# Hybrid conformer and gated-recurrence layer: the MLP's first product with tokens stationary, its results turned by VectorE and through memory

## The chip, the core and the metric

The kernel runs on one core of one Trainium2 chip. The metric is device microseconds of one execution. The engines are called here as the profile calls them: PE is TensorE's matmuls, PEld its weight loads, DVE is VectorE, ACT is ScalarE, POOL is GpSimd, SP is SyncE, which here only issues transfers.

## The reference

One layer over 256 latent tokens of width 2048, with 256 context tokens ahead of them: a modulation from the conditioning vector, a convolution branch and a gated recurrence branch that are merged and projected, and then an MLP. The change touches the MLP alone:

```python
D_MODEL = 2048
SEQ = 256
D_FF = 4 * D_MODEL

def sq_relu_mlp(h, w1, w2):
    return jnp.square(jax.nn.relu(h @ w1)) @ w2

h2 = modulate(rms_norm(x, norm_pre_mlp[l]), sh_f, sc_f)
x = x + ga_f * rms_norm(sq_relu_mlp(h2, mlp_w1[l], mlp_w2[l]), norm_post_mlp[l])
```

h is 256 x 2048, w1 is 2048 x 8192, w2 is 8192 x 2048, all float32.

## The kernel before

**Products.** Every product is made of three, to keep float32's precision: an operand is split into a high part and the rest (hi and lo), and hi*hi, hi*lo and lo*hi are summed in PSUM. Activations are split once (`split`, L237); weights arrive as pages of 128 x 1024 (512 KB) through SP's queue (`fetch`, L85) into 5 raw buffers, ACT makes whi (L123) and DVE makes wlo (L126), each in 4 buffers. `Stream.next` keeps up to 4 pages ready ahead of PE. A raw buffer, a whi or a wlo is written again only when its reader is done.

**Two forms of a product.** In `blocks` (with `mm2`, L252 and L254) a 128 x 128 piece of the weights is stationary and the tokens move: a page is eight matmuls of 512 columns (whi against hi and lo of the 256 tokens side by side) and eight of 256 columns (wlo against hi). The result has features on the partitions, as the next product needs it for its stationary operand; its two halves of 256 columns still have to be added (`totals`: an ACT copy at L228, a DVE add at L229, for each 128 features). In `tokens` (with `mm3r`, through L185) 128 x 128 pieces of the activations are stationary and the weights move: a page is twelve matmuls of 512 columns (3 terms, 2 blocks of 128 tokens called tb, 2 halves of the page called j). The result has tokens on the partitions. Four banks fill at once; of the last three pages (LAST) each bank is finished in turn, so that the banks end one after another.

**The MLP's order.** The 8192 hidden features are four quarters q of 2048. `up(q)` makes a quarter's hidden values and `down(q)` multiplies them by their rows of w2; each takes 32 pages. `up` is of the `blocks` form, `down` of the `tokens` form. The evacuation of `up` (`ev`) takes 256 features at a time: `totals`, relu on ACT (L988), square on ACT (L990), `split` into pages hidh and hidl. The first 1024 features of `up(0)` are an exception: `first_up` makes them in the `tokens` form, page by page behind the projection that delivers its input. Their values stand with tokens on the partitions in two pages called hidden (L1202), and the generator `turn_hidden` turns them with 16 PE transposes (L1215) and splits them, while the rest of `up(0)` runs.

**Background work.** Generators are pushed on a list, and `pump` runs a step of up to three of them after each page; `finish` runs one to its end. In the MLP a generator of another kind, `gain_row`, makes rows of gains; its two transfers (L1276, L1277) are issued from POOL. The products for it (`gemv`, L1236 on DVE) come as extra raw pages, one after every sixth page of w1 and w2, up to 32.

**Buffers and order.** Pages of 128 x 1024 float32 come from one pool of 30 (`page`). Each engine, and each queue of transfers, works its own list of instructions in order; a planner makes that list when the kernel is built, from the order of the code and from what it takes to be ready, and inserts all waits. `issue_after` only orders instructions on one engine.

Of the kernel before, what the change touches and what calls it, by code (L numbers as in the profile page):

```python
# [8 lines left out]
F32 = mybir.dt.float32  # L9
F32R = mybir.dt.float32r  # L10
I32 = mybir.dt.int32
U8 = mybir.dt.uint8
AF = mybir.ActivationFunctionType
ALU = mybir.AluOpType

P = 128
T = 256
D = 2048
KT = D // P
# [7 lines left out]
TW = 1024  # L27
# [7 lines left out]
PB = 4  # L35
# [16 lines left out]
class Stream:  # L52


    def __init__(self, kn):
        self.kn = kn
        self.items = []
        self.done = 0
        self.behind = []
        self.ready = collections.deque()  # L60
        self.raws = collections.deque()
        self.dma = None
# [74 lines left out]
class Kernel:  # L137
    def __init__(self, ctx, tc, a, out):
        self.tc = tc
        self.nc = tc.nc  # L140
        self.a = a
        self.out = out
        self.wp = ctx.enter_context(tc.tile_pool(name="wp", bufs=1))
        self.pg = ctx.enter_context(tc.tile_pool(name="pg", bufs=1))
        self.sp = ctx.enter_context(tc.tile_pool(name="sp", bufs=1))
        self.cp = ctx.enter_context(tc.tile_pool(name="cp", bufs=1))
        self.ps = ctx.enter_context(tc.tile_pool(name="ps", bufs=1, space=bass.MemoryType.PSUM))
        self.bg = collections.deque()
        self.his, self.los = [], []
        self.credit = 0.0  # L150
        self.queued = None
# [213 lines left out]
    def run(self):  # L365
        nc, a = self.nc, self.a
# [125 lines left out]
        first = self.cp.tile([P, 1], F32, name="first")  # L492
# [9 lines left out]
        for i in range(2):  # L502
            ps = self.bank()
# [160 lines left out]
        for c in range(8):  # L664
            part = sums(c, self.last3)
            ps = self.bank()
            for t in range(KP // 2):
                st.fetch_to(FETCH)
                w = st.whole()
                for k2 in range(2):  # L670
                    k = 2 * t + k2
                    g = 32 * (k % 4)
# [69 lines left out]
        for h in range(NH):  # L742
            accs = []
            for d in range(2 * (h > 0)):
                accs.append(self.bank())
                for hf in range(2):
                    hi, lo = st.next()
                    for k8 in range(8):
                        k = 8 * hf + k8
# [18 lines left out]
        uh = self.pages(2, F32, "uh")  # L768
# [201 lines left out]
        h2x = self.operand(h2)  # L970
        y2 = self.pages(4, F32, "y2")
        hid = {}
        begun = self.first_up(yp, xr, A2, mv[:, 0], h2)
        self.tokens(zx, ev_wo, 1.4, end=True, pre=pre_wo, begin=begun)


        def up(q):
            uh_, ul_ = [], []
            hid[q] = (uh_, ul_)

            def ev(b, acc):
                if b % PB == 0:
                    uh_.append(self.page(F32R, "hidh"))
                    ul_.append(self.page(F32R, "hidl"))
                if isinstance(acc, list):
                    acc = self.totals(acc, self.small(512, "sum"))
                r = self.small(512, "relu")
                nc.scalar.activation(out=r, in_=acc, func=AF.Relu)  # L988
                sq = self.small(512, "rsq")
                nc.scalar.activation(out=sq, in_=r, func=AF.Square)  # L990
                self.split(sq, self.at(uh_, b, 2), self.at(ul_, b, 2))
            if q == 0:
                for n in range(2):
                    uh_.append(self.page(F32R, "hidh"))
                    ul_.append(self.page(F32R, "hidl"))
                turned = self.push(self.turn_hidden(uh_, ul_))
            self.blocks(16 if q else 8, h2x, KT, ev, 1.4, first=0 if q else 8)
            if q == 0:
                self.finish(turned)

        def gained2(yp, tb, c, s=slice(0, 512)):
            nc.vector.tensor_tensor(self.cut(yp, tb, c)[:, s], self.cut(y2, tb, c)[:, s], gain_row(1, c)[:, s], op=ALU.mult)

        def down(q):
            uh_, ul_ = hid[q]

            def ev(tb, c, acc):
                y = self.cut(y2, tb, c)
                if q == 0:
                    nc.scalar.copy(out=y, in_=acc)  # L1010
                    return
                end = (tb, c) == (1, 3) and q == 3
                nc.vector.tensor_tensor(y, acc[0] if end else acc, y, op=ALU.add)
                if q < 3:
                    return
                if not end:
                    self.squares(ssq[:, 4 * tb + c:4 * tb + c + 1], y)
                    gained2(yp, tb, c)
                else:

                    for h in range(2):
                        s, o = slice(h * T, (h + 1) * T), ssq[:, 7 + h:8 + h]
                        nc.vector.tensor_tensor(y[:, s], acc[1 + h], y[:, s], op=ALU.add)
                        if h == 0:
                            self.squares(o, y[:, s])
                            gained2(yp, tb, c, s)
                        else:
                            nc.vector.scalar_tensor_tensor(self.small(T, "junk"), y[:, s], 1.0, y[:, s], op0=ALU.mult, op1=ALU.mult, accum_out=o)
                if c < 3:
                    return  # L1030
                r = self.rstd_tok(ssq[:, 4 * tb:4 + 5 * tb])[0]
                if end:
                    with self.tc.issue_after(self.summed.ins):
                        gained2(yp, tb, c, s)
                for i in range(4):
                    x1, o = self.cut(xr, tb, i), self.out[tb * P:(tb + 1) * P, i * 512:(i + 1) * 512]
                    if end and i == 0:

                        halves = [(self.bank()[:, :T], slice(h * T, (h + 1) * T)) for h in range(2)]
                        for ps, s in halves:  # L1040
                            nc.tensor.matmul(ps, v["ident"], x1[:, s], start=True, stop=False)
                        self.warm(10)
                        diag = self.small(P, "diag")
                        nc.scalar.activation(out=diag, in_=v["ident"], func=AF.Copy, scale=r)
                        for ps, s in halves:
                            nc.tensor.matmul(ps, diag, self.cut(yp, tb, i)[:, s], start=False, stop=True)
                        for ps, s in halves:
                            nc.scalar.copy(out=x1[:, s], in_=ps)
                            nc.scalar.dma_start(o[:, s], x1[:, s])
                        continue  # L1050
                    for s in (slice(0, T), slice(T, 512)) if end and i in (1, 3) else (slice(0, 512),):
                        nc.vector.scalar_tensor_tensor(x1[:, s], self.cut(yp, tb, i)[:, s], r, x1[:, s], op0=ALU.mult, op1=ALU.add)
                        nc.sync.dma_start(o[:, s], x1[:, s])
            yp = self.pages(4, F32, "gained") if q == 3 else None
            self.tokens(lambda k: (self.at(uh_, k), self.at(ul_, k)), ev, 1.4, end=q == 3, halves=q == 3)

        for q in range(4):
            up(q)
            down(q)

    def first_up(self, y, x, A, B, h2):
# [4 lines left out]
        nc, st = self.nc, self.stream  # L1066
        ident = self.v["ident"]
# [50 lines left out]
        t = {}  # L1118
# [32 lines left out]
        for k in range(2):  # L1151
            a, b = cols(k)
# [18 lines left out]
        for k in range(FIRST, KT):  # L1171
            pair = 4 if k == FIRST else k + 2 if k % 2 == 0 else KT
            if pair < KT:
                ps = self.bank()
# [19 lines left out]
                        self.add(0, slice(0, T), False)  # L1194
            self.pump(1.4)

        self.hidden = [self.page(F32, "hidden") for tb in range(2)]
        for tb in range(2):
            for j in range(2):
                r = self.small(512, "relu")  # L1200
                nc.scalar.activation(out=r, in_=accs[tb][j], func=AF.Relu)
                nc.scalar.activation(out=self.hidden[tb][:, j * 512:(j + 1) * 512], in_=r, func=AF.Square)  # L1202

    def split_at(self, src, parts, t):
        return self.split(src, parts[:, t], parts[:, T:][:, t])

    def turn_hidden(self, uh, ul):

        for _ in range(3):
            yield None  # L1210
        for b in range(0, 8, 2):
            ps = self.bank()
            for j in range(2):
                for tb in range(2):
                    self.nc.tensor.transpose(out=ps[:, j * T + tb * P:j * T + (tb + 1) * P], in_=self.hidden[tb][:, (b + j) * P:(b + j + 1) * P], identity=self.v["ident"])  # L1215
            self.split(ps, self.at(uh, b, 2), self.at(ul, b, 2))
            yield 0.7
            yield None

    def warm(self, n=WARM):  # L1220

        ps = self.bank()
        for _ in range(n):
            self.pe(self.nc.tensor.matmul, ps[:, :P], self.ones_r, self.ones_r, start=True, stop=True)

    def gemv(self, raw, i, k, h):

# [396 lines left out]
```

## Time and profile before

| | |
|---|---|
| median of 3 runs | 1643.5 us (1642.47 to 1644.42) |
| the profiled execution | 1644.45 us |
| its span in the profile | 1642.7 us, so 1.75 us lie around it |
| granted clock of TensorE | full in all slices |
| PE / DVE / ACT busy | 99% / 71% / 49% of the span |

A page of the profile gives busy times of the engines, the chain of work that ended last, and groups of instructions by source line with a mean duration and what ended the idle time before them. Matmuls are pipelined, so a matmul's own duration is longer than its share of PE's time; what one costs is read from the distance between starts, or from a stretch divided by its count.

### The profile page before, as it was taken

Reading aid. Unit: us, or ns where it says so; the run is one execution under the profiler, and the core shown is the slowest. Engines: PE = TensorE matmul, PEld = TensorE weight load, DVE = VectorE, ACT = ScalarE, POOL = GpSimd, SP = SyncE. Lnnn points to the kernel's source line nnn. Section 1 sums busy time; section 2 is a strip of 40 time slices with the busy share of each in tenths; the row PEclk is TensorE's granted clock in tenths of the full one; section 3 lists DMA queues with packets and bytes.
Section 4 is the critical chain, followed back from the end, with each engine's and each line's share of the span. In section 5 each row is a group of like instructions: output and inputs, shape, how many; then the busy total and the mean of one; then the engine's idle time right before and its main releaser. Section 6 shows DMA issues by size and latency. Waiting matters only on the chain.

```text
span 1642.7 us, 22019 instructions
## 1 busy us (share of the span) xinstructions
PE 1627.8 (99%) x8211; PEld 1359.2 (83%) x8211; DVE 1163.1 (71%) x1703; ACT 799.9 (49%) x1142; POOL 8.1 (0%) x18
## 2 busy tenths in 40 slices
PE   8999999999999999999999999999999999999998
PEld 6668888888988888888888888888888888888887
DVE  7777777778868889967887766456655665566555
ACT  6553444443554444653446665445544554346543
POOL 0000000000000000000000000000000000000000
PEclk9999999999999999999999999999999999999999
DMA  9998954444656556688887376677667667666553
GB/s 375 389 395 292 318 163 149 154 142 141 204 185 227 189 187 210 228 277 294 317 291 269 136 233 204 212 237 240 219 205 232 233 214 215 232 219 195 190 192 116
DMA packets 103771, 374.47 MB, mean 228 GB/s; under 512 B 11632, under 2 KB 12400, under 8 KB 103664
## 3 DMA queue, kind: packets, MB, share of 16 engines
q1 hardware_dynamic: 102096, 368.60, 66.4%
q0 software_dynamic: 1280, 4.21, 0.9%
q8 instruction: 64, 1.05, 0.3%
q14 instruction: 43, 0.35, 0.1%
q10 hardware_dynamic: 288, 0.26, 0.0%
HBM read 370.93 MB, written 2.10 MB: 227 GB/s over the span
## 4 chain that ended last, share of the span: by engine, by line
PE 93%; DVE 2%; DMA 2%; ACT 1%; issue 1%; SPq 0%; ACTq 0%; DVEq 0%
PE bank L185 62%; PE bank L252 18%; PE bank L254 9%; PE bank L1396 2%; DMA raw<-wpw 1%; DVE wlo L126 1%; DMA x<-ctx 1%; DMA rawpage<-wm 1%; ACT whi L123 0%; PE bank L1427 0%; PE bank L1438 0%; PE bank L1436 0%; DVE gacc L1236 0%; SPq L498 0%; PE bank L1419 0%
## 5 line engine op out<-in xcount | busy, mean ns | idle before, releaser
L126 DVE TENSOR_TENSOR wlo<-raw,whi 128x1024 fp32r<-128x1024 f32 x488 | 594.7, 1224 | 356.2 <-ACT whi L123 348.4
L123 ACT ACTIVATE whi<-raw 128x1024 fp32r<-128x1024 f32 x488 | 513.4, 1059 | 577.7 <-PE bank L185 322.9
L185 PE MATMUL bank<-whi,h 128*128 128x512 f32 x1264 | 396.6, 392 | 0.8 <-ACT h L629 0.5
L252 PE MATMUL bank<-h,whi 128*128 128x512 f32 x1280 | 322.4, 394 | 0.0
L185 PEld LDWEIGHTS bank<-whi,h 128*128 128x128 f32 x1264 | 237.3, 188 | 50.9 <-DVE h L1085 0.7
L252 PEld LDWEIGHTS bank<-h,whi 128*128 128x128 f32 x1280 | 230.7, 189 | 41.3
L185 PE MATMUL bank<-wlo,h 128*128 128x512 f32 x632 | 246.9, 391 | 0.7 <-DVE wlo L126 0.5
L185 PE MATMUL bank<-whi,hidh 128*128 128x512 f32 x503 | 195.3, 388 | 0.0
L185 PE MATMUL bank<-wlo,hidh 128*128 128x512 f32 x503 | 195.3, 388 | 0.0
L185 PE MATMUL bank<-whi,hidl 128*128 128x512 f32 x503 | 195.3, 388 | 0.0
L254 PEld LDWEIGHTS bank<-h,wlo 128*128 128x128 f32 x1280 | 174.6, 190 | 12.6
L254 PE MATMUL bank<-h,wlo 128*128 128x256 f32 x1280 | 178.5, 283 | 0.0
L185 PE MATMUL bank<-h,whi 128*128 128x512 f32 x512 | 164.7, 403 | 0.0
L185 PEld LDWEIGHTS bank<-wlo,h 128*128 128x128 f32 x632 | 118.8, 188 | 26.5 <-DVE wlo L126 2.4
L185 PEld LDWEIGHTS bank<-whi,hidh 128*128 128x128 f32 x503 | 94.5, 188 | 19.3
L185 PEld LDWEIGHTS bank<-whi,hidl 128*128 128x128 f32 x503 | 94.5, 188 | 19.2
L185 PEld LDWEIGHTS bank<-wlo,hidh 128*128 128x128 f32 x503 | 94.5, 188 | 19.2
L185 PEld LDWEIGHTS bank<-h,whi 128*128 128x128 f32 x512 | 92.1, 189 | 21.4 <-issue 5.9
L185 PE MATMUL bank<-h,wlo 128*128 128x512 f32 x256 | 100.2, 391 | 0.0
L1236 DVE SCALAR_TENSOR_TENSOR gacc<-raw,silu_c,gacc 128x1024 f32<-128x1024 f32 x60 | 76.8, 1279 | 0.0
L1249 DVE SCALAR_TENSOR_TENSOR raw<-raw,silu_row 128x1024 f32<-128x1024 f32 x64 | 76.5, 1220 | 0.0
L185 PEld LDWEIGHTS bank<-h,wlo 128*128 128x128 f32 x256 | 48.1, 188 | 10.5 <-DVE wlo L126 0.3
(246 smaller groups left out, 1363.0 us busy)
## 6 DMA issues: line engine op xcount, KB each, us to landing
raw<-w SPq DMA_DIRECT2D x256, 512.0 KB, 4.3
raw<-wi SPq DMA_DIRECT2D x172, 512.0 KB, 4.4
raw<-wmt SPq DMA_DIRECT2D x64, 512.0 KB, 4.3
raw<-wm SPq DMA_DIRECT2D x64, 512.0 KB, 4.5
rawpage<-wm SPq DMA_DIRECT2D x48, 512.0 KB, 8.8
raw<-wo SPq DMA_DIRECT2D x32, 512.0 KB, 4.7
raw<-wmd SPq DMA_DIRECT2D x16, 512.0 KB, 8.6
raw<-who SPq DMA_DIRECT2D x16, 512.0 KB, 5.1
```

What stands on the lines that cost most here:

```text
L123: kn.his.append(nc.scalar.activation(out=hi, in_=raw, func=AF.Copy))
L126: kn.los.append(nc.vector.tensor_tensor(lo, raw, hi.bitcast(F32), op=ALU.subtract))
L185: ins = fn(*args, **kw)
L252: nc.tensor.matmul(bank, w[0][:, cut(i)], x(k)[2], start=(k == 0), stop=False)
L254: nc.tensor.matmul(bank[:, T:], w[1][:, cut(i)], x(k)[0], start=False, stop=(k == nk - 1))
L1236: nc.vector.scalar_tensor_tensor(acc, raw, s, acc, op0=ALU.mult, op1=ALU.add)
L1249: nc.vector.scalar_tensor_tensor(raw, raw, 1.0, self.srow, op0=ALU.mult, op1=ALU.mult, accum_out=self.dot[:, 32 * j + b:32 * j + b + 1])
L1396: nc.tensor.matmul(ps[:, b * P:(b + 1) * P], w, r, start=True, stop=True)
```

## The change

`up(q)` is written in the `tokens` form throughout: the pieces of h2 are stationary and w1's pages move, laid out as w2's are. Its four evacuations for each 1024 features do relu and square on ACT, as before, and then `turn_blocks`: a DVE transpose of a 128 x 512 piece in blocks of 32 x 32, written into a page called turned. When both pages (one for each tb) of 1024 features are there, `turn_hidden` is pushed. Its first step, `swapped`, sends each page to a buffer in DRAM (one transfer of 512 KB) and fetches it back in four transfers of 128 KB, each to 32 partitions in runs of 1 KB, which puts the 32 x 32 blocks in their places; all ten are issued from POOL. After five empty steps it splits the fetched pages into hi and lo, in a step for each tb (two ACT and two DVE instructions of 128 x 512). For the first 1024 features of a quarter this runs during the second half of `up(q)`, and `up` finishes it at its end. For the second 1024 it runs beside the first pages of `down(q)`, which finishes it ahead of its page 7; the features are needed from page 8 on. `first_up` uses the same way, and the PE transposes are gone.

```diff
+        turns = {0: [self.push(self.turn_hidden(hid, 0, self.hidden))]}
+
         def up(q):
-            uh_, ul_ = [], []
-            hid[q] = (uh_, ul_)
-
-            def ev(b, acc):
-                if b % PB == 0:
-                    uh_.append(self.page(F32R, "hidh"))
-                    ul_.append(self.page(F32R, "hidl"))
-                if isinstance(acc, list):
-                    acc = self.totals(acc, self.small(512, "sum"))
+            def ev(tb, c, acc):
+                if c % 2 == 0:
+                    self.hidden[tb] = self.page(F32, "turned")
                 r = self.small(512, "relu")
                 nc.scalar.activation(out=r, in_=acc, func=AF.Relu)
                 sq = self.small(512, "rsq")
                 nc.scalar.activation(out=sq, in_=r, func=AF.Square)
-                self.split(sq, self.at(uh_, b, 2), self.at(ul_, b, 2))
-            if q == 0:
...
-            self.blocks(16 if q else 8, h2x, KT, ev, 1.4, first=0 if q else 8)
-            if q == 0:
-                self.finish(turned)
+                self.turn_blocks(self.hidden[tb], c % 2, sq)
+                if (tb, c % 2) == (1, 1):
+                    turns.setdefault(q, []).append(self.push(self.turn_hidden(hid, q, list(self.hidden))))
+            self.hidden = [None, None]
+            self.tokens(h2x, ev, 1.4, groups=2 if q else 1)
+            self.finish(turns[q][0])
...
+            def pre(g, k):
+
+                if (g, k) == (0, 7):
+                    self.finish(turns[q][1])
...
+    def turn_blocks(self, page, j, src):
+        out = page[:, :TW].rearrange("p (j b r) -> p b j r", j=4, b=8)[:, 4 * j:4 * j + 4]
+        self.nc.vector.transpose(out=out, in_=src.rearrange("p (b j r) -> p b j r", b=4, j=4))
...
+    def turn_hidden(self, hid, q, pages):
...
+        for tb in range(2):
+            back.append(self.swapped(pages[tb]))
+        for _ in range(5):
             yield None
-        for b in range(0, 8, 2):
-            ps = self.bank()
-            for j in range(2):
-                for tb in range(2):
-                    self.nc.tensor.transpose(...)
-            self.split(ps, self.at(uh, b, 2), self.at(ul, b, 2))
-            yield 0.7
-            yield None
+        new = [[self.page(F32R, f"hid{n}") for i in range(2)] for n in "hl"]
+        for p, pages in zip(parts, new):
+            p.extend(pages)
+        for tb in range(2):
+            for n in range(2):
...
+                with self.tc.issue_after(self.his[-1].ins):
+                    self.split(src, hi, lo)
+            yield 1.4
...
+    def swapped(self, page):
+        there = self.dr.tile([P, TW], F32, name="there", tag="there", bufs=4)
+        nc.gpsimd.dma_start(there, page[:, :TW])
+        back = self.page(F32, "back")[:, :TW]
+        for j in range(4):
+            nc.gpsimd.dma_start(back[32 * j:32 * j + 32].rearrange("c (i f) -> c i f", i=4),
+                                there[:, j * T:(j + 1) * T].rearrange("(i c) f -> c i f", i=4))
+        return back
```

## Rows read from the trace of the kernel before

**Rows 1.** The page: busy us (share of the span) and instructions of each engine.
```profile
PE 1627.8 (99%) x8211; PEld 1359.2 (83%) x8211; DVE 1163.1 (71%) x1703; ACT 799.9 (49%) x1142; POOL 8.1 (0%) x18
```
**Rows 2.** Who PE waited for, longest first: us in total, times, longest.
```profile
PE bank L185 <- DVE silu_c L391: 4.5, 1, 4.5
PE bank L185 <- DMA x<-x: 2.3, 1, 2.3
```
**Rows 3.** Stages: the rest of up(0), down(0), up(1), down(2), up(3).
```profile
core 0: us, PE busy (x) PEld busy (x) DVE busy (x) ACT busy (x) POOL busy (x), PEclk, DMA share, GB/s
969.18:1015.62 46.44, 46.44 (x273) 41.09 (x272) 28.60 (x32) 29.16 (x43) 0.00 (x0) 1.00 0.67 217
1015.62:1102.69 87.07, 87.07 (x386) 72.14 (x385) 43.48 (x38) 37.97 (x43) 1.05 (x2) 1.00 0.69 223
1102.69:1192.05 89.36, 89.36 (x513) 78.71 (x512) 56.99 (x61) 51.50 (x71) 0.00 (x0) 1.00 0.70 224
...
1369.41:1456.48 87.07, 87.07 (x387) 72.12 (x385) 48.05 (x45) 33.96 (x36) 0.00 (x0) 1.00 0.67 217
1456.48:1546.76 90.28, 90.28 (x517) 79.45 (x516) 57.20 (x64) 52.16 (x72) 0.00 (x0) 1.00 0.63 205
```
**Rows 4.** The tile hidden: PE transposes (ns min/median/max, first and last start).
```profile
L1215 PE MATMUL bank<-pack,hidden x16: 272/273/274, 980.3 to 990.4; 128*128 128x128 f32 x16
```
**Rows 5.** Groups by line in the whole span: busy us, mean ns, idle before.
```profile
L229 DVE TENSOR_TENSOR sum<-bank,terms 128x256 f32<-128x256 f32 x72 | 30.1, 418 | 5.3 <-ACT terms L228 5.3
...
L237 DVE TENSOR_TENSOR hidl<-rsq,hidh 128x512 fp32r<-128x512 f32 x28 | 19.3, 691 | 0.3 <-ACT hidh L237 0.3
L988 ACT ACTIVATE relu<-sum 128x512 f32<-128x512 f32 x28 | 17.7, 633 | 36.7 <-DVE sum L229 36.7
...
L990 ACT ACTIVATE rsq<-relu 128x512 f32<-128x512 f32 x28 | 17.3, 617 | 0.2
```
**Rows 6.** Timeline where down(1) ends and up(2) begins: start, duration, engine, line.
```profile
1276.17 0.69 DVE L1013 TENSOR_TENSOR y<-bank,y 128x512 f32<-128x512 f32 x1 [1.16 <-PE bank L185]
...
1278.21 0.69 DVE L1013 TENSOR_TENSOR y<-bank,y 128x512 f32<-128x512 f32 x1 [1.35 <-PE bank L185]
...
1278.89 2.96 ACT L123 ACTIVATE whi<-raw 128x1024 fp32r<-128x1024 f32 x3 [5.74 <-PE bank L185]
...
1279.98 2.36 DVE L126 TENSOR_TENSOR wlo<-raw,whi 128x1024 fp32r<-128x1024 f32 x2 [1.08 <-ACT whi L123]
1280.05 1.98 PE L252 MATMUL bank<-h,whi 128*128 128x512 f32 x8
1280.28 0.50 POOL L1276 DMA_DIRECT2D bias<-bgain  x1 [187.68 <-PE bank L185]
1280.79 0.55 POOL L1277 DMA_DIRECT2D gain<-gain  x1
...
1282.26 0.69 DVE L1013 TENSOR_TENSOR y<-bank,y 128x512 f32<-128x512 f32 x1
```
**Rows 7.** Line L1277 from 1270 to 1290 us: its one transfer, 512 KB.
```profile
DMA to landing us min/median/max: 4.9/4.9/4.9
```
**Rows 8.** Line L855, four transfers of 512 KB from POOL.
```profile
DMA to landing us min/median/max: 4.6/5.9/7.7
```
**Rows 9.** The page's list of transfers: KB each, median us from issue to landing.
```profile
gain<-gain POOLq DMA_DIRECT2D x4, 512.0 KB, 6.1
...
out<-xr SPq DMA_DIRECT2D x4, 128.0 KB, 2.4
```
**Rows 10.** Two stretches of 5 us behind the end of down(1), columns as in the stages.
```profile
1281.00:1286.00 5.00, 5.00 (x31) 4.47 (x30) 4.27 (x6) 3.05 (x4) 0.34 (x1) 1.00 0.70 240
1286.00:1291.00 5.00, 5.00 (x31) 4.38 (x30) 3.93 (x4) 1.80 (x3) 0.00 (x0) 1.00 1.02 413
```
**Rows 11.** POOL's timeline in the MLP.
```profile
1081.39 0.50 POOL L1276 DMA_DIRECT2D bias<-bgain  x1 [268.13 <-PE bank L185]
```
**Rows 12.** Line L1234, the one DVE operation of the MLP with a scalar operand.
```profile
L1234 DVE TENSOR_SCALAR gacc<-raw,silu_c x4: 747/750/757, 679.4 to 1216.8; 128x1024 f32<-128x1024 f32 x4
```

More of the change, by code (lines that the diff above doesn't have):

```diff
@@ L146, in __init__ @@
         self.cp = ctx.enter_context(tc.tile_pool(name="cp", bufs=1))
+        self.dr = ctx.enter_context(tc.tile_pool(name="dr", bufs=1, space=bass.MemoryType.DRAM))
         self.ps = ctx.enter_context(tc.tile_pool(name="ps", bufs=1, space=bass.MemoryType.PSUM))
@@ L990, in ev @@
                 nc.scalar.activation(out=sq, in_=r, func=AF.Square)
-                self.split(sq, self.at(uh_, b, 2), self.at(ul_, b, 2))
-            if q == 0:
[L993 to L996, printed above, removed]
-            self.blocks(16 if q else 8, h2x, KT, ev, 1.4, first=0 if q else 8)
-            if q == 0:
-                self.finish(turned)
+                self.turn_blocks(self.hidden[tb], c % 2, sq)
[4 more added lines that the diff above has]
+            self.finish(turns[q][0])
         def gained2(yp, tb, c, s=slice(0, 512)):
@@ L1054, in down @@
             yp = self.pages(4, F32, "gained") if q == 3 else None
-            self.tokens(lambda k: (self.at(uh_, k), self.at(ul_, k)), ev, 1.4, end=q == 3, halves=q == 3)
+            self.tokens(lambda k: (self.at(uh_, k), self.at(ul_, k)), ev, 1.4, end=q == 3, halves=q == 3, pre=pre)
         for q in range(4):
@@ L1195, in first_up @@
             self.pump(1.4)
-        self.hidden = [self.page(F32, "hidden") for tb in range(2)]
+        self.hidden = [self.page(F32, "turned") for tb in range(2)]
         for tb in range(2):
@@ L1201, in first_up @@
                 nc.scalar.activation(out=r, in_=accs[tb][j], func=AF.Relu)
-                nc.scalar.activation(out=self.hidden[tb][:, j * 512:(j + 1) * 512], in_=r, func=AF.Square)
+                sq = self.small(512, "rsq")
+                nc.scalar.activation(out=sq, in_=r, func=AF.Square)
+                self.turn_blocks(self.hidden[tb], j, sq)
     def split_at(self, src, parts, t):
         return self.split(src, parts[:, t], parts[:, T:][:, t])
-    def turn_hidden(self, uh, ul):
-        for _ in range(3):
-            yield None
-        for b in range(0, 8, 2):
-            ps = self.bank()
-            for j in range(2):
-                for tb in range(2):
-                    self.nc.tensor.transpose(out=ps[:, j * T + tb * P:j * T + (tb + 1) * P], in_=self.hidden[tb][:, (b + j) * P:(b + j + 1) * P], identity=self.v["ident"])
-            self.split(ps, self.at(uh, b, 2), self.at(ul, b, 2))
-            yield 0.7
-            yield None
+    def turn_blocks(self, page, j, src):
+        out = page[:, :TW].rearrange("p (j b r) -> p b j r", j=4, b=8)[:, 4 * j:4 * j + 4]
+        self.nc.vector.transpose(out=out, in_=src.rearrange("p (b j r) -> p b j r", b=4, j=4))
+    def turn_hidden(self, hid, q, pages):
+        nc = self.nc
+        parts = hid.setdefault(q, ([], []))
+        back = []
+        for tb in range(2):
+            back.append(self.swapped(pages[tb]))
+        for _ in range(5):
+            yield None
+        new = [[self.page(F32R, f"hid{n}") for i in range(2)] for n in "hl"]
[3 more added lines that the diff above has]
+            for n in range(2):
+                src = back[tb].rearrange("p (i b r) -> p b i r", i=4, b=8)[:, PB * n:PB * n + PB]
+                hi, lo = (pages[n][:, :TW].rearrange("p (b t i r) -> p b t i r", b=PB, t=2, i=4)[:, :, tb] for pages in new)
+                with self.tc.issue_after(self.his[-1].ins):
+                    self.split(src, hi, lo)
+            yield 1.4
     def warm(self, n=WARM):
@@ L1224, in warm @@
             self.pe(self.nc.tensor.matmul, ps[:, :P], self.ones_r, self.ones_r, start=True, stop=True)
+    def swapped(self, page):
+        nc = self.nc
+        there = self.dr.tile([P, TW], F32, name="there", tag="there", bufs=4)
[5 more added lines that the diff above has]
+        return back
     def gemv(self, raw, i, k, h):
@@ L1575, in rows @@
         return w.reshape(n, P, 2, TW).transpose(2, 0, 1, 3).reshape(-1, P, TW)
-    def both(w):
-        n = w.shape[0] // P
-        return np.concatenate([w[:, :TW].reshape(n, P, TW), cb(w[:, TW:])], axis=0)
     def row(w):
@@ L1611 @@
         "wo": rows(f(w_out)[0]),
-        "w1": np.concatenate([both(w1[:, :D]), cb(w1[:, D:])], axis=0),
+        "w1": np.concatenate([rows(w1[:, i * D:(i + 1) * D]) for i in range(4)], axis=0),
         "w2": np.concatenate([rows(w2[i * D:(i + 1) * D]) for i in range(4)], axis=0),
```

## Prediction

> **What bounds the kernel now.** I read the page first: PE is busy for 1627.8 us, 99% of the span, DVE 71%, ACT 49% [rows 1]. Then PE's waits: the two longest, 4.5 and 2.3 us, lie at the very start of the kernel, and every later one is 0.5 us or less [rows 2]. Then the stages of the MLP one by one: in each of them PE is busy for the whole stretch, at the full clock, with DVE at 50 to 64% of it, ACT at 39 to 63% and the transfers at 63 to 70% of theirs [rows 3]. So in the MLP the time is PE's, and only two things change it: what PE's own instructions take, and whether anything makes PE wait where it never waits now.
>
> **What PE saves.** A quarter of `up` and a quarter of `down` are both 32 pages with the same products, in the two forms. down(0) and down(2) take 87.07 us each, 2.721 us for a page of twelve matmuls, 226.7 ns for one. up(1) takes 89.36 us, 2.793 us for a page [rows 3]. The columns that move are the same (8 x 512 + 8 x 256 against 12 x 512); the difference is sixteen instructions against twelve. So up(1), up(2) and up(3) lose 2.29 us each, 6.87 us together (up(3)'s 90.28 holds a product for a gain row, which stays). The rest of up(0) is 16 pages and the 16 PE transposes, 46.44 us [rows 3, 4]; in the new form it is 16 x 2.721 = 43.53 us, so 2.91 us less, of which half of 2.29 is the form and 1.76 the transposes. Together **9.78 us**. The price of the new form is not a guess by analogy: `down` runs it on the same chip with the same shapes. I take it whole; below it could be nothing (a rival), above it nothing speaks for more.
>
> **What the other engines get.** DVE loses 56 adds of `totals` at 418 ns (23.4 us) and ACT 56 copies; DVE gets 32 transposes of 128 x 512. The trace has none. The nearest rows of that size are 691 ns (a subtraction with two inputs [rows 5]) and, halved, the 750 ns of a scalar operation on twice the size, 375 ns [rows 12]; at the upper end I put twice the former, 1.38 us, since an output in strides may cost more. I take 0.69: 22.1 us, as much as goes away. Even at 1.38 us DVE stays under 70% in a stage of 87 us, so this is hidden by PE's work. Relu, square and the splits stay as many (relu 633 ns, square 617 [rows 5]) but for four more splits. The evacuation is no wait for PE: four banks fill while the other four are emptied, as in `down`. POOL, nearly idle (8.1 us [rows 1]), gets 80 issues of some 0.53 us. The transfers get 16 pages out and back, 16.8 MB over some 670 us, 25 GB/s on the 205 to 224 that flow there [rows 3]; the weights have five raw buffers and four pages ready in front of PE, some 10 us of cover, so a landing later by a microsecond or two costs nothing.
>
> **What is new on PE's path.** The first 1024 features of each quarter are turned while PE works 16 pages of `up`, 43.5 us; that covers any price below. The second 1024 are not: they exist when `up(q)` ends, and `down(q)` wants them at its page 8. There are four such places. Let 0 be the end of `up`. I build the time L at which the last fetched piece lands.
>
> The end of down(1) shows what an end of this form looks like [rows 6]. Banks end 2.04 us apart (1276.17 to 1278.21 were such evacuations), so tb 0's second bank ends at -4.1, and its page is turned after relu, square and transpose (1.25 + 0.69) at about -2 to -1. tb 1's last bank ends at 0. ACT has three whi queued to 1281.85, that is 1.8 after the end, and DVE two wlo to 2.3 (which is why the last y stands at 1282.26). So tb 1's page is ready between 2.2 and 3.8; I take 3.8.
>
> A POOL issue takes 0.50 to 0.55 us. The price of a transfer is best read at the very same place: the 512 KB that POOL issued at 1280.79 landed after 4.9 us [rows 6, 7]. The medians elsewhere are 6.1 [rows 9] and 5.9, the extremes of the latter group 4.6 and 7.7 [rows 8]; a 128 KB transfer of 1 KB runs took 2.4 where nothing else ran [rows 9]. Weights do run here: the transfers are busy 0.70 and then all of the time in the two stretches behind the boundary [rows 10]. I take 4.9 for each step, also for the four pieces back, which are 512 KB together; bounds 2.4 and 7.7.
>
> Two orders on POOL are possible. If the second page goes out before the first comes back: 3.8 + 4.9 = 8.7 out, the last of four pieces issued at 10.3, L = 15.2. If POOL waits for the first page's return before it issues the second: -1 + 4.9 = 3.9, four issues to 6.0, out at 10.9, last piece issued 12.5, **L = 17.4**; with 6.1 a step 21.0; with 7.7 a step 25.8; with 2.4 a step about 10. What the code's order says is the second; I take it.
>
> When is L too late? PE reaches page 8 at 8 x 2.72 = 21.8, and wants tb 1's lo at 23.6 at the earliest; it is there at L + 0.63 + 0.69, so L may be 22.2. A tighter limit is ACT's queue: the splits of tb 1 stand behind the whi of page 8 and ahead of that of page 9. While ACT waits for L, page 9 waits too: two splits (1.26), whi (1.0), wlo (1.2) make L + 3.5, and PE wants that wlo at 24.7. So **L may be 21.2**, and each microsecond beyond costs PE one, four times. The taken 17.4 leaves 3.8 us; the stall is nothing. Its cover is PE's pages 0 to 8 of `down`, and if that cover is gone the price is (L - 21.2) x 4.
>
> One rule of the Trainium skill speaks against POOL as the issuer. The row first: at 1280.28 and 1280.79, in the middle of two wlo that kept DVE busy from 1279.98 to 1282.34, POOL's issues took 0.50 and 0.55 us [rows 6], so a DVE subtraction with two inputs doesn't hold them. The Trainium skill (SBUF — State Buffer, section SBUF: two separate sides) says that a transfer issued from GpSimd has its descriptors written by GpSimd, which is locked out while VectorE runs an operation that takes both ports, and advises the other queues. Whether the transpose is such an operation it doesn't say there, and no row here can show it. By the row the sum stays; by the rule, were it so, see the third rival.
>
> **The rivals.**
>
> *1. The round trip comes late (the other side).* With each step at 7.7 us, as one row of four on POOL had it [rows 8], L = 25.8 and PE stalls 4.6 us at each of four ends: 1633.7 + 18.4 = 1652. It decides at L = 22.8 (gain within 0.2%) and at 24.5 (slower by over 0.2%): a step of 6.7 or 7.3 us in the serial order. For it: the transfers are full right behind the boundary [rows 10]. Against it: 4.9 was measured in that very stretch [rows 7]. Chances: L up to 21.2 see the forecast; 21.2 to 22.8, still faster (1634 to 1640), 0.09; 22.8 to 24.5, 0.07; above, 0.11.
>
> *2. A queue on POOL.* POOL works in order, and a transfer for a gain row once waited there 268 us until PE freed a page [rows 11]. A page on its way out that stands behind such a wait stalls PE until the page is free: behind the one that ended at 1081.39, 1081.39 - 1015.62 - 21 = some 45 us, 1679. Against it: the last such issue stood right at a boundary and held nothing [rows 6]. Chance 0.04.
>
> *3. The transposes hold POOL's issues.* Two of them, for tb 1, run when POOL issues the first page's return. At 0.69 each L is 18.8 and nothing changes; at 1.38 each with steps of 6.1, L = 23.8, a stall of 2.6 x 4 and 1644, no gain. As the third number needs both bounds at once, it has 0.03, taken as faster, since most of its cases are at 1634 to 1640. It is the rule above that gives this case.
>
> *4. The change doesn't do what it says:* the new form takes 2.79 us a page here too, and only the 1.76 us of the PE transposes is gained: 1641.7. Against it stand two stages of the same form with the same price [rows 3]. Chance 0.04.
>
> **How the numbers follow.** The profiled execution took 1644.45 us, 1.75 beyond its span; less 9.78 that is 1634.7. It lies 0.95 above the median of the runs, 1643.5, and so I predict 1643.5 - 9.78 = **1633.7 us** for the median, with 0.62 for this case and its own range of 1632.5 to 1635 (the runs spread by 1 us to each side). A measurement of this kernel tells about 0.2%, 3.3 us, from no change. Faster: 0.62 + 0.09 + 0.03 = 0.74. Same: 0.07 + 0.04 = 0.11. Slower: 0.11 + 0.04 = 0.15. The range reaches into the cases with a partly late return and takes in the fourth rival: 1632.5 to 1642, which leaves out slower and a part of the same, less than 0.2.
>
> **What would show it.** After the change each of up(1) to up(3) should take 87.1 us (up(3) 88.0) and the rest of up(0) 43.5, PE busy throughout. The transposes on DVE should read 0.4 to 1.4 us, most likely 0.7. PE's waits should stay free of any for a split of the fetched pages or for the whi and wlo of pages 8 to 10 of `down`. POOL's transfers near the four ends should land in 5 to 6 us, the last at 15 to 21 after `up`'s end. The prediction is wrong if `down` grows from 87.1 to 90 or more in all four quarters (a late return), if one quarter grows by tens of microseconds (a queue on POOL), or if `up` stays at 89.

## The result and the profile after

The changed kernel takes 1649.45 us (median of 11 runs, 1643.26 to 1653.83) against 1643.5 before: 1.0033 of the time, 95% interval 1.0021 to 1.0046. It is slower by a third of a per cent, where 1633.7 was forecast, and its runs spread by 10 us where those of before spread by 2. The profiled execution took 1651.03 us, its span is 1649.3.

The first line of the page after, beside [rows 1]:
```profile
PE 1624.1 (98%) x7747; PEld 1336.4 (81%) x7747; DVE 1162.8 (71%) x1679; ACT 780.6 (47%) x1086; POOL 52.0 (3%) x98
```
PE has less to do and is less busy: the span grew by work that is not PE's. The stages say where. The view is that of [rows 3], after the change: up(0) with its first half, down(0), up(1), down(1), down(2), up(3), and down(3) to the end.
```profile
core 0: us, PE busy (x) PEld busy (x) DVE busy (x) ACT busy (x) POOL busy (x), PEclk, DMA share, GB/s
920.75:1012.81 92.06, 91.75 (x419) 75.32 (x419) 63.55 (x92) 56.84 (x93) 6.04 (x11) 1.00 0.70 225
1012.81:1104.60 91.79, 89.24 (x385) 73.10 (x384) 47.80 (x44) 40.73 (x47) 4.91 (x9) 0.98 0.73 233
1104.60:1191.64 87.04, 87.04 (x385) 72.11 (x384) 51.52 (x48) 43.32 (x51) 6.03 (x11) 1.00 0.77 250
1191.64:1284.74 93.10, 89.88 (x389) 73.75 (x388) 55.45 (x56) 38.00 (x42) 5.99 (x11) 0.98 0.72 235
...
1371.78:1463.80 92.02, 89.11 (x385) 73.06 (x384) 52.45 (x51) 36.80 (x40) 5.99 (x11) 0.98 0.73 238
1463.80:1551.77 87.97, 87.97 (x389) 72.86 (x388) 51.98 (x51) 43.77 (x52) 6.01 (x11) 1.00 0.74 229
1551.77:1649.30 97.53, 91.07 (x421) 75.43 (x419) 58.27 (x71) 41.49 (x58) 4.92 (x9) 0.99 0.57 182
```
`up` went as forecast: 89.36 became 87.04 in up(1) (and in up(2), which repeats it), 90.28 became 87.97 in up(3), 6.95 us together. But `down`, whose products the change doesn't touch, became longer: 87.07 to 91.79 and 92.02 in down(0) and down(2), and 5.1 and 1.6 us more in down(1) and down(3), which took before:
```profile
1192.05:1280.05 88.00, 88.00 (x390) 72.89 (x389) 51.04 (x50) 35.11 (x38) 0.00 (x0) 1.00 0.66 215
...
1546.76:1642.70 95.94, 90.53 (x422) 75.58 (x420) 53.69 (x65) 38.50 (x54) 0.00 (x0) 1.00 0.48 159
```
That is 16.4 us together. The span grew by 6.6; 16.4 less 6.6 and 6.95 leaves 2.8 us that were gained ahead of down(0), close to the 2.91 of the sum for up(0) (the start of down(0) varies by 1.7 us between the runs below). So the saving is there, and well over one and a half times as much is lost at four places in `down`.

PE's waits name the places. Before, none in the MLP was over 0.5 us [rows 2]; now the longest group of the whole kernel is this:
```profile
PE bank L186 <- ACT hidh L238: 9.7, 4, 3.2
```
There are four pauses, one in each `down`, some 23 us after its start: PE waits for the split of the fetched pages, at page 8. The split waits for the last piece, as ACT's timeline in down(1) shows (starts at 1191.64):
```profile
1211.85 0.61 ACT L238 ACTIVATE hidh<-back 128x512 fp32r<-128x512 f32 x1
1217.01 0.63 ACT L238 ACTIVATE hidh<-back 128x512 fp32r<-128x512 f32 x1 [4.54 <-DMA back<-there]
```
And POOL's timeline of the trip that ends there:
```profile
1190.06 0.56 POOL L1246 DMA_DIRECT2D there<-turned  x1 [25.14 <-DVE turned L1212]
1193.51 2.19 POOL L1249 DMA_DIRECT2D back<-there  x4 [2.89 <-issue]
1196.56 0.56 POOL L1246 DMA_DIRECT2D there<-turned  x1 [0.87 <-DVE turned L1212]
1206.98 2.18 POOL L1249 DMA_DIRECT2D back<-there  x4 [9.86 <-ACT whi L123]
1209.15 0.51 POOL L1303 DMA_DIRECT2D bias<-bgain  x1
```
From issue to landing these took, in the same order, with the weights that SP issued from 1194 to 1201 us in the last line:
```profile
DMA to landing us min/median/max: 2.9/2.9/2.9
...
DMA to landing us min/median/max: 4.3/7.5/8.3
...
DMA to landing us min/median/max: 9.8/9.8/9.8
...
DMA to landing us min/median/max: 6.0/7.1/8.3
...
DMA to landing us min/median/max: 8.0/8.0/8.0
...
DMA to landing us min/median/max: 8.8/9.3/9.8
```
The first page goes out in 2.9 us, while the weights rest at the end of `up`. Then the weights start again, and most transfers take 6 to 10 us: a page out 9.8, a piece of 128 KB up to 8.3, and even a transfer of 4 KB for the gain row 8.0. It was issued behind the pieces on POOL's queue, and landed 0.2 us after the last of them. The weights themselves, which took 3.2 to 4.7 us behind the same boundary before, need 9.3. The last piece was issued at 1208.61 and took 8.30, so it lands at 1216.91, that is L = 25.3 us after the end of `up`. The stretches of 5 us in which this happens show why:
```profile
1199.00:1204.00 5.00, 5.00 (x24) 4.14 (x23) 1.79 (x2) 0.32 (x1) 0.00 (x0) 1.00 1.02 278
1204.00:1209.00 5.00, 5.00 (x24) 4.15 (x23) 3.11 (x3) 3.36 (x4) 2.02 (x4) 1.00 1.01 394
1209.00:1214.00 5.00, 5.00 (x24) 4.14 (x23) 3.02 (x3) 2.15 (x3) 1.23 (x3) 1.00 0.99 238
```
For 15 us the 16 DMA engines are busy all of the time (the column ahead of the last), where [rows 10], behind the end of a `down`, had one such stretch of 5.

What a pause costs is more than its length. The four pauses are 9.7 us and the loss is 16.4. The other 6.6 us are in PE's busy time, which in down(1) grew from 88.00 to 89.88. TensorE's granted clock (the column ahead of the DMA share) fell behind the pause that ended at 1217.69:
```profile
1216.00:1218.00 2.00, 0.31 (x1) 0.31 (x2) 0.84 (x1) 0.99 (x2) 0.00 (x0) 0.90 1.02 373
1218.00:1220.00 2.00, 2.00 (x5) 1.34 (x5) 2.00 (x4) 2.00 (x4) 0.00 (x0) 0.50 1.01 401
1220.00:1222.00 2.00, 2.00 (x8) 1.57 (x7) 2.00 (x5) 0.67 (x2) 0.00 (x0) 0.74 0.21 84
1222.00:1224.00 2.00, 2.00 (x11) 1.60 (x10) 1.80 (x3) 1.06 (x1) 0.00 (x0) 1.00 0.00 0
```
0.50 is the lower of the two levels, 1.2 GHz: from 1218 to 1220 PE starts 5 matmuls, from 1222 to 1224, at the full clock, 11. The shares 0.90, 0.50 and 0.74 leave out 0.86 x 2 = 1.7 us of the full clock.

DVE's transposes, the one operation that no trace had shown, were as taken (0.69):
```profile
L1212 DVE STREAM_TRANSPOSE turned<-rsq 128x512 f32<-128x512 f32 x32 | 22.6, 708 | 22.5 <-ACT rsq L987 22.0 <-ACT rsq L1202 0.4
```

### The profile page after: what moved, and what is told of

Same layout as the page of the kernel before. It is cut to its first block, busy times and chain, and to the rows that moved or that the text cites. A ratio compares the mean times of both kernels' runs of the same rounds, so it can differ in the third digit from the quotient of the medians.

```text
span 1649.3 us, 21098 instructions
## 1 busy us (share of the span) xinstructions
PE 1624.1 (98%) x7747; PEld 1336.4 (81%) x7747; DVE 1162.8 (71%) x1679; ACT 780.6 (47%) x1086; POOL 52.0 (3%) x98
## 4 chain that ended last, share of the span: by engine, by line
PE 85%; DMA 7%; DVE 3%; ACT 2%; issue 1%; SPq 0%; POOL 0%; ACTq 0%; DVEq 0%; POOLq 0%
PE bank L186 73%; PE bank L253 5%; PE bank L255 3%; PE bank L1423 2%; DMA back<-there 2%; DVE wlo L126 1%; DMA there<-turned 1%; DMA raw<-wpw 1%; DMA rawpage<-wm 1%; ACT whi L123 1%; DMA raw<-wf 1%; DMA x<-ctx 1%; DMA raw<-w 1%; PE bank L1454 0%; PE bank L1465 0%
## 5 line engine op out<-in xcount | busy, mean ns | idle before, releaser
L126 DVE TENSOR_TENSOR wlo<-raw,whi 128x1024 fp32r<-128x1024 f32 x488 | 592.7, 1222 | 311.9 <-ACT whi L123 305.6
L186 PE MATMUL bank<-whi,h 128*128 128x512 f32 x2160 | 673.2, 391 | 0.8 <-ACT h L630 0.5
L186 PEld LDWEIGHTS bank<-whi,h 128*128 128x128 f32 x2160 | 405.5, 188 | 86.0 <-DVE h L1084 0.7
L186 PE MATMUL bank<-wlo,h 128*128 128x512 f32 x1080 | 421.3, 390 | 0.6 <-DVE wlo L126 0.5
L186 PEld LDWEIGHTS bank<-wlo,h 128*128 128x128 f32 x1080 | 203.0, 188 | 43.7 <-DVE wlo L126 2.6
L186 PE MATMUL bank<-h,whi 128*128 128x512 f32 x512 | 164.7, 403 | 0.0
L186 PEld LDWEIGHTS bank<-h,whi 128*128 128x128 f32 x512 | 92.1, 189 | 21.4 <-issue 5.9
L253 PE MATMUL bank<-h,whi 128*128 128x512 f32 x384 | 97.8, 397 | 0.0
L253 PEld LDWEIGHTS bank<-h,whi 128*128 128x128 f32 x384 | 69.1, 189 | 12.3
L186 PEld LDWEIGHTS bank<-h,wlo 128*128 128x128 f32 x256 | 48.1, 188 | 10.6 <-DVE wlo L126 0.3
L255 PEld LDWEIGHTS bank<-h,wlo 128*128 128x128 f32 x384 | 52.4, 190 | 3.9
L255 PE MATMUL bank<-h,wlo 128*128 128x256 f32 x384 | 53.5, 282 | 0.0
```

Source lines behind the costliest of these rows:

```text
L126: kn.los.append(nc.vector.tensor_tensor(lo, raw, hi.bitcast(F32), op=ALU.subtract))
L186: ins = fn(*args, **kw)
L253: nc.tensor.matmul(bank, w[0][:, cut(i)], x(k)[2], start=(k == 0), stop=False)
L255: nc.tensor.matmul(bank[:, T:], w[1][:, cut(i)], x(k)[0], start=False, stop=(k == nk - 1))
```

## Experiments

The theory behind the first four: the form saves what was summed; the loss is the second trip of each quarter, which lands late, and the clock behind PE's pause. Rivals: the new form, the transposes or the splits' place in ACT's queue cost something of their own; the order on POOL alone makes the trip late; a pause costs its length alone.

**No transfers.** `swapped` returns the turned page itself, so the blocks stay where they are:
```diff
-        there = self.dr.tile([P, TW], F32, name="there", tag="there", bufs=4)
-        nc.gpsimd.dma_start(there, page[:, :TW])
...
-        return back
+        return page[:, :TW]
```


> The changed kernel without the transfers: the splits read the turned pages directly, so the 32 x 32 blocks are not put in their places (left out: the exchange of blocks). If the late return and what PE's pause costs behind it are all that went wrong, the sum of the prediction stands alone here: up at 87.0, down at 87.1 and 88.0 us, no pause at page 8, 1633.7 us (1633 to 1635). If the new form of up, the transposes on VectorE or the place of the splits in ScalarE's queue cost something of their own, it stays above 1637.

1633.76 us (1632.94 to 1635.0), 0.9936 of before (0.9921 to 0.9951). All else of the change is in it: the form, the transposes, the splits in strides, their place in ACT's queue. down(0), up(1) and down(3) to the end:
```profile
1013.24:1100.28 87.04, 87.04 (x386) 72.10 (x384) 47.88 (x44) 40.86 (x47) 1.05 (x2) 1.00 0.69 230
1100.28:1187.32 87.04, 87.04 (x386) 72.10 (x384) 51.60 (x48) 43.66 (x51) 0.00 (x0) 1.00 0.70 224
...
1537.35:1633.20 95.85, 90.49 (x421) 75.54 (x419) 58.34 (x71) 41.72 (x58) 0.00 (x0) 0.99 0.51 165
```
Each `up` and each `down` takes what the sum took for it, so the sum for PE was right, as far as the spread of the runs can tell, and nothing else in the change costs time that these runs show. The transfers alone cost 1649.45 - 1633.76 = 15.7 us. This kernel also shows the room that the trip had. Behind the end of up(1), in four stretches of 5 us, the weights alone keep the DMA engines busy so:
```profile
1187.32:1192.32 5.00, 5.00 (x24) 4.14 (x23) 4.74 (x6) 4.22 (x6) 0.00 (x0) 1.00 0.47 137
1192.32:1197.32 5.00, 5.00 (x24) 4.14 (x23) 3.97 (x4) 2.12 (x2) 0.00 (x0) 1.00 0.91 300
1197.32:1202.32 5.00, 5.00 (x24) 4.14 (x23) 4.91 (x7) 4.41 (x7) 0.00 (x0) 1.00 0.88 304
1202.32:1207.32 5.00, 5.00 (x24) 4.14 (x23) 3.82 (x5) 2.77 (x4) 0.00 (x0) 1.00 0.59 213
```
Of these 20 us 5.75 are free (1 less each share, times 5). The trip's 2.1 MB at the 413 GB/s of the full stretch in [rows 10] would be an estimate of 5.1 us, nearly all of it.

**Both pages out first.** The second page is sent before the first one's pieces are fetched; the number and the sizes stay:
```diff
+        for tb in range(2):
+            theres.append(self.dr.tile([P, TW], F32, name="there", tag="there", bufs=4))
+            outs.append(nc.gpsimd.dma_start(theres[tb], pages[tb][:, :TW]))
+        with self.tc.issue_after(outs[1].ins):
+            for tb in range(2):
+                back.append(self.swapped(theres[tb]))
```


> Both pages are sent out before any piece is fetched back (order on POOL alone). If the second page's way out is slow because it is queued behind the first page's eight-microsecond return on POOL's own queue, it now lands in 3 to 6 us instead of 9.5, the last piece comes at 18 to 21 after the end of up instead of 25, and the kernel takes 1634 to 1640. If the transfers are slow because the engines are full with the weights that catch up, the order changes little: last piece at 23 to 25, 1644 to 1650.

1637.6 us, 0.9960 (0.9945 to 0.9974): faster than before. The second page out and the second four pieces in down(1):
```profile
DMA to landing us min/median/max: 6.0/6.0/6.0
...
DMA to landing us min/median/max: 7.1/8.2/8.9
```
The page out gained 3.8 us by not standing behind the pieces; the pieces took as long as in the changed kernel or longer. The last landed 22.0 to 23.4 us after the ends of `up`, not 18 to 21, and PE's pauses shrank to 0.1 to 0.9 us. Order is a part of the lateness, then, but the transfers stay slow.

**PE kept busy.** 20 small matmuls of no use ahead of page 8:
```diff
             def pre(g, k):
                 if (g, k) == (0, 7):
                     self.finish(turns[q][1])
+                if (g, k) == (0, 8):
+                    self.warm(20)
```


> The changed kernel with 20 small matmuls of no use ahead of page 8 of each down, so that PE is busy in the time in which it else waits. If part of the loss is the lower clock behind the pause (about 2 us of the 4.7 to 5.1 that a down lost), the clock stays full and the kernel takes 1641 to 1645 with the same landing times. If the clock behind the pause costs nothing of its own, the same 1648 to 1650, or more.

1650.89 us, 1.0039 (1.0024 to 1.0054): the expected gain did not come. The stages tell why. Here are down(0) and down(1), and in down(1) PE's pause and the first of the small matmuls behind it:
```profile
1012.52:1101.82 89.30, 89.30 (x406) 74.30 (x404) 47.89 (x44) 40.87 (x47) 4.93 (x9) 1.00 0.75 240
1188.86:1285.70 96.84, 92.27 (x410) 75.82 (x408) 55.62 (x56) 37.99 (x42) 6.00 (x11) 0.98 0.71 226
...
1216.22 0.50 PE L186 MATMUL bank<-whi,hidh 128*128 128x512 f32 x1 [4.53 <-ACT hidh L238]
...
1220.42 0.44 PE L186 MATMUL bank<-ones_r 128*128 128x128 f32 x3
```
down(0) lost 2.3 us at the full clock, down(2) 2.5, but there the last pieces also landed earlier than in the changed kernel (L = 23.8 and 24.5). In down(1) the small matmuls had come to stand behind the gain row's on PE, 4 us behind the end of the pause, and covered nothing; the last piece landed at L = 26.6, and PE paused for 4.5 us for its split, with the lower clock behind it. Once more without down(1), with 22 small matmuls:
```diff
+                if (g, k) == (0, 8) and q != 1:
+                    self.warm(22)
```


> The changed kernel with 22 small matmuls of no use ahead of page 8 of down(0), down(2) and down(3), not of down(1), where the first try shifted the order of the gain row's matmuls. If the lower clock behind a pause is a cost of its own, down(0) and down(2) lose 2.4 to 2.8 us, what the small matmuls or the wait take, in place of 4.7 and 5.0, at the granted clock of 1.0, down(1) still loses 5, and the kernel takes some 4 us less than the changed one: 1645. If a pause costs its length alone, down(0) and down(2) lose as much as before.

1648.97 us, 1.0032 (1.0019 to 1.0045), where 1645 was expected; it can't be told apart from the changed kernel. down(0) and down(1), and the clock behind down(1)'s pause:
```profile
1013.40:1104.01 90.61, 90.10 (x408) 74.39 (x407) 47.81 (x44) 40.77 (x47) 4.92 (x9) 1.00 0.74 236
1191.05:1282.78 91.73, 88.66 (x390) 72.53 (x388) 55.36 (x56) 38.00 (x42) 5.99 (x11) 1.00 0.73 239
...
1216.00:1218.00 2.00, 1.06 (x4) 0.58 (x4) 1.97 (x3) 2.00 (x4) 0.00 (x0) 1.00 1.02 408
```
down(0) lost 3.6 us, more than the 2.4 to 2.8 expected, as its last piece landed still later (25.5), and down(2) 3.8. In these stages the clock was full and the loss 1 us less than the 4.7 and 5.0 of the changed kernel, in spite of the later landing. The untouched down(1) surprised: a pause of 2.7 us, no lower clock, a loss of 3.8 and not 5. So a lower clock, where it comes, costs 1 to 2 us, as the 1.7 worked out above; but it doesn't come behind every pause, and the time of the whole kernel didn't show the difference, against runs that spread by several microseconds.

**Half of the change.** Only the first 1024 features of each quarter in the new form and through memory, where 16 pages of `up` lie over the trip:
```diff
+            if q:
+                self.hidden = [None, None]
+                self.tokens(h2x, ev_first, 1.4, groups=1)
+            self.blocks(8, h2x, KT, ev, 1.4, first=8)
             self.finish(turns[q][0])
```


> Only the first 1024 features of each quarter in the new form and through memory; the second 1024 by the old form, which needs no turning. The trip then lies under 16 pages of up. If the uncovered trip is the whole loss: saved are 3 x 1.145 us for the form and 1.76 us for the PE transposes, 5.2 us, 1638.3 us (1637.5 to 1639.5), down at 87.1 and no pause. If the transfers hurt by loading the memory system anywhere, or the transposes by loading VectorE, 1641 or more.

1639.37 us, 0.9969 (0.9956 to 0.9982). down(0) and the second half of up(1):
```profile
1012.56:1099.62 87.06, 87.06 (x386) 72.08 (x385) 43.48 (x38) 37.98 (x43) 0.00 (x0) 1.00 0.68 223
...
1143.14:1187.81 44.67, 44.67 (x258) 39.33 (x256) 32.48 (x37) 28.10 (x41) 6.00 (x11) 1.00 0.87 286
```
While the trip runs the DMA engines are busy at 0.87, and PE never waits. The transfers are as slow as elsewhere (the second pages take 8.1 to 9.4 us to go out) and cost nothing where they are covered.

**No weights beside the second trip.** Pages 7 to 15 of w2 in each quarter are not loaded (an earlier page is used in their place, so the results are not the layer's):
```diff
         ap, fn, paged = self.items[n]
+        if n in self.skip:
+            self.raws.append(self.last)
+            return
```


> The changed kernel without the loads of pages 7 to 15 of w2 in each quarter (left out: these weights; an earlier page is used again), so that hardly any other transfer runs while the second trip of a quarter is on its way. If the engines that are full with weights make the trip slow, the page out takes 3 us, the pieces back 3 to 4, the last lands 12 to 15 us after up's end, and PE does not pause: 1634. If POOL's own queue or the runs of 1 KB are slow by themselves, the pieces still take 6 to 8 us, the second page out 8 or more, and PE pauses as before.

1634.91 us in two runs, 0.9945 (0.9927 to 0.9963). The second four pieces of down(1), and the 5 us in which they land:
```profile
DMA to landing us min/median/max: 4.3/4.3/4.4
...
1205.00:1210.00 5.00, 5.00 (x23) 3.95 (x22) 3.59 (x5) 4.15 (x6) 0.00 (x0) 1.00 0.36 113
```
4.3 us and not 6.0 to 8.3, over the four quarters 2.9 to 5.3. The second page out was as slow as before (9.3 to 9.8), as the weights ahead of page 7 and the first pieces were still on their way then. The last piece landed at 19.7 to 22.2, later than the 12 to 15 expected, but soon enough. With the same runs of 1 KB and the same issues from POOL, the pieces of the second page took some 3 us less than beside the weights, and PE never waited. So it is the weights on the same DMA engines that make the trip too slow; how much of the 2.9 to 5.3 us that are left belongs to the runs of 1 KB isn't shown.

**A trip by columns.** A trip for each 512 features and not for each block of tokens. The banks end in the order of columns (`pairs`), a page holds both token blocks of 512 features, and the second 512 are wanted four pages later:
```diff
-                if (tb, c % 2) == (1, 1):
-                    turns.setdefault(q, []).append(self.push(self.turn_hidden(hid, q, list(self.hidden))))
+                if tb == 1:
+                    turns.setdefault(q, []).append(self.push(self.turn_hidden(hid, q, self.hidden[c % 2], NONES[c % 2])))
...
+            self.tokens(h2x, ev, 1.4, groups=2 if q else 1, pairs=True)
...
+        out = page[:, :TW].rearrange("p (j t b r) -> p t b j r", j=4, t=2, b=4)[:, tb]
```


> The changed kernel with a trip for each 512 features instead of each block of 128 tokens: the banks end in the order of columns, a turned page holds both token blocks of 512 features, and its trip starts when its two banks are done. The first 512 are ready some 2 us before up ends and are wanted at page 8 (21.8 us), the second 512 are ready at 4 to 5 us and are wanted at page 12 (32.7 us). Sizes, number and order of the transfers stay. If only the late landing costs time, it takes the 1633.8 us of the kernel without transfers (1633 to 1635.5), with no pause of PE. If the trips also slow the weights enough to make PE wait, or if the clock falls for another reason, 1637 or more.

1639.92 us (1636.82 to 1642.23), 0.9974 (0.9963 to 0.9984): faster than before, but not what was expected. In the profile all stages are as without transfers but down(1), with one pause of 1.9 us. Here DVE's timeline, the stage, and the clock behind the pause:
```profile
1209.33 1.21 DVE L1305 TENSOR_TENSOR gacc<-gacc,bias 1x1024 f32<-1x1024 f32 x1 [2.00 <-DMA bias<-bgain]
1210.47 1.27 DVE L239 TENSOR_TENSOR hidl<-back,hidh 128x512 fp32r<-128x512 f32 x2
...
1185.77:1277.53 91.76, 89.84 (x389) 73.96 (x388) 55.44 (x56) 38.11 (x42) 5.99 (x11) 0.98 0.72 239
...
1213.00:1215.00 2.00, 2.00 (x6) 1.63 (x5) 1.69 (x3) 0.46 (x1) 0.00 (x0) 0.50 0.31 59
```
The pieces that PE wanted had landed. DVE stood at an add for the gain row, which waited for its 4 KB behind a trip on POOL, and the split stood behind the add. The runs spread by 5 us and the profiled one, at 1637.25, was among the fastest, so the median holds more than this one pause shows.

**By columns, and the gain row later.** The generator of the MLP's gain rows takes nine empty steps more ahead of that add:
```diff
-        yield None
+        for _ in range(1 + 9 * i):
+            yield None
```


> The kernel with a trip for each 512 features, and the generator of the gain rows of the MLP waits nine pages longer before VectorE adds the bias. In the kernel with trips by columns PE's one pause of 1.9 us, in down(1), stood behind a split that stood behind this add, and the add waited for a transfer of 4 KB queued on POOL behind a trip. If that is what was left, down(1) takes 88.0 us instead of 91.8 and the kernel 1633.8 (1633 to 1635.5). If it was the trips themselves, 1637 or more as before.

1634.45 us (1633.9 to 1634.61), 0.9944 (0.9932 to 0.9957). down(0), down(1), down(2):
```profile
1012.47:1099.51 87.04, 87.04 (x386) 72.07 (x385) 47.89 (x44) 40.84 (x47) 4.92 (x9) 1.00 0.75 246
...
1186.55:1274.65 88.10, 88.10 (x389) 72.74 (x388) 55.53 (x56) 38.11 (x42) 5.99 (x11) 1.00 0.76 248
...
1361.69:1448.73 87.04, 87.04 (x385) 72.07 (x384) 52.42 (x51) 36.94 (x40) 5.99 (x11) 1.00 0.77 252
```
The last pieces land 23.4 to 24.9 us after the ends of `up`, little earlier than the 23.5 to 25.4 of the changed kernel, and PE doesn't wait: what was mended is when they are wanted, and what stands behind the gain row's transfer, not how long the trip takes. This kernel does the whole change and beats both; it is within 0.7 us of the one without transfers.

## Why the prediction was wrong

**What bounds the kernel, and what PE saves: right.** The 9.78 us were read from stages of the same form, and the kernel without transfers took 1633.76 us; that it hit 1633.7 so closely is luck, as its runs spread by 2 us. The rival that the form saves nothing is out. DVE's cost was taken rightly too (0.71 us a transpose); `totals` and the transposes cancel.

**The step that failed: "I take 4.9 for each step ... bounds 2.4 and 7.7".** The price of a transfer was read from one transfer of 512 KB that ran beside the weights behind the end of a `down`. The trip is ten transfers, 2 MB out and back, into the stretch in which the weights catch up. Counted as the prediction counts, the first page's way out took 2.9 us, the second page's 9.3 to 9.8, and the last piece 8.3 to 8.8 in three quarters and 7.0 in the fourth. In down(1) the second page was issued at 4.9 and landed at 14.7, the last piece was issued at 17.0 and landed at 25.3. L was 25.0, 25.3, 25.4 and 23.5, where 17.4 was taken. The upper bound, a single row of 7.7, was passed by the second page in all four trips and by the last piece in three. A row of one transfer holds for one more; here the added bytes had to be put beside the room that the stretch had left, 5.75 of 20 us in the kernel without transfers for an estimated 5.1. The kernel without the weights beside the second trip shows it from the other side: L of 19.7 to 22.2 and no pause.

The serial order on POOL was forecast rightly, but the second page went out at 4.9 and not at 6.0, since the first had landed sooner than taken. What kept it then was DVE: its last transpose stood behind wlo, so the page was ready at 4.6 and not at 3.8.

**The rival that came true** is the first, with 0.11: it gave L = 25.8, 4.6 us at each of four ends and 1652; measured were 4.7, 5.1, 5.0 and 1.6. Two terms of it were wrong and cancelled. The limit of 21.2 came from ACT's queue, with the splits ahead of the whi of page 9; in the trace the second token block's split is the last thing that PE waits for, and the data's own limit, 22.2, held. L less 22.2 is 2.8, 3.1, 3.2 and 1.3 us; PE's idle time in the four stages is 2.6, 3.2 and 2.9, and in down(3) 1.1 more than before. The kernel without the weights, with L up to 22.2, lost 0.3 us at most in a `down`. And a microsecond late was priced at one, while the lower clock behind a pause added 1 to 2 us at each of three.

**The queue on POOL** came the other way round. No page stood behind the gain row's transfer; the gain row's transfer, early before, stood behind the trip, and held DVE and through it a split. In the changed kernel the late pieces hid this; in the kernel by columns it was all that was left.

**The transposes hold POOL's issues: no run shows it.** The issues took 0.53 to 0.57 us, also the six in the changed kernel that overlap a transpose, by 0.1 to 0.3 us only. So the rule that the Trainium skill (SBUF — State Buffer, section SBUF: two separate sides) gives for two-port operations didn't decide here; none of these runs shows whether the transpose is one.

The Trainium skill (DMA: Bandwidth & Descriptors, section Anatomy of one DMA — SWDGE (gpsimd) path) gives for a transfer issued from GpSimd about 2.0 us and its bytes at 436 GB/s, an estimate of 3.2 us for 512 KB. The trace agrees for a page that went out with no weights on their way (2.9) and not for one among the weights (9.8), and the latter decided this case.

**What stays open:** why the lower clock followed a pause of 1.9 us in one kernel and not one of 2.7 in another, and which of the unprofiled runs of the kernel by columns paused how long. The changed kernel, cut by tokens, was not run with the gain row's add moved later; in down(1) its pause ended with the split of a piece that had landed 0.7 us earlier, so little speaks for a gain there, but it isn't shown.

## What to carry to other kernels

A trip through memory is priced by the DMA engines' room in that stretch, with its own bytes added, and not by the time that one transfer took there; every transfer queued behind it gets late too, even one of 4 KB. When a round trip is late, look at when each part of it is wanted before making it faster: the same slow trip cost 15.7 us cut by tokens, 6.2 cut by columns, where the parts become ready and are consumed in the same order, and 0.7 when the add that stood behind its queue was moved as well. And price a pause of PE above its length, since the clock may fall behind it.

## What was not expected of the hardware

A page of 512 KB to memory took 2.9 us with no weights on their way and 9.8 us where the DMA engines were full; a transfer of 4 KB took 8.0 us behind others on its queue. The granted clock fell to 0.50 behind pauses of 1.9 and 3.2 us, which cost 1.7 us of the full clock behind the latter, and stayed at 1.00 behind one of 2.7 us.
